# Stick-breaking attention on one core: which engine rounds log(1+e^z) to the matmul format

## Chip, core and metric

The kernel runs on one core of one Trainium2 chip. The metric is the device time of one execution, in microseconds (us). TensorE is called PE, VectorE DVE, ScalarE ACT, GpSimd POOL and SyncE SP.

## What is computed

A two-layer block on one sequence of 512 tokens with 1024 features, in float32. The first layer (pooling and gating mixer, cross attention to 256 memory rows, convolutional FFN of width 2816) ends in a norm. The second layer projects to q, k, v (8 heads of 64) and to a gated convolution of 31 taps over 512 channels, joins attention and convolution in one output product, and ends in a second FFN. The part that matters here is its attention:

```python
z = einsum("bqhd,bkhd->bhqk", qb, kb) * scale           # strictly causal, s < t
log_beta = log_sigmoid(z)
log_one_minus = where(mask, log_sigmoid(-z), 0.0)       # = -log(1 + e^z)
tail = cumsum(log_one_minus, reverse) - log_one_minus   # sum over s < j < t
weights = where(mask, exp(log_beta + tail), 0.0)
out = einsum("bhqk,bkhd->bqhd", weights, vb)
```

## The kernel before

Activations lie with features on the 128 partitions and the 512 tokens along the free axis. Every product runs as three matmuls in a 32-bit matmul format (`fp32r`): an operand is split into `hi`, its rounding to that format, and `lo`, the rest, and hi·hi, hi·lo and lo·hi are added in PSUM (`mm3`, L122 to L125). Weights come in units of 1 MB by SP and are split by ACT (L195) and DVE (L196).

The attention works on four head pairs `hp` = 0 to 3. Each pair has three score tiles `n` = 0, 1, 2, 2x384, 2x384 and 2x512 columns wide (768, 768 and 1024 elements per partition), so there are twelve steps (hp, n). A step has two halves.

- `sticks(hp, n)`: PE writes the scores to a pair of PSUM banks (L774, and the mask at L779). ACT takes Abs, Exp and Ln (L782 to L784), DVE adds max(z, 0) (L785, the "merge"; one operand in PSUM, one in SBUF), and the result log(1+e^z) is split: `hi` by ACT (L131 through `copy_split`), `lo` by DVE (L132, the subtraction, which reads `ex` and `hi` from SBUF).
- `breaks(hp, n)`: PE adds the running sums onto the scores (L798, L801), reading `hi` and `lo`; ACT takes Exp (L803). `gather(hp)` multiplies with the values (L813), and ACT and DVE split the result into `G`.

The same stretch has filler on DVE: the convolution (L832) is done as 120 "taps", one `scalar_tensor_tensor` over 128x512 each, with both tensors in SBUF. `conv_norm` (L877) needs all taps, adds the squares with PE (L882, L895, L904) and gives the operand of the second half of the output product. The first half, `attended` (L941), is 96 matmuls that use `G`.

Each engine runs its instructions strictly in one order. That order is not the order of the source: a scheduler places the instructions of all engines when the program is built, from its own estimate of what each costs, within the data dependences and a few `issue_after` marks. If an operation moves to another engine, the scheduler can place its neighbours differently, too.

```python
        dve.scalar_tensor_tensor(ex, z, 0.0, ex, ALU.max, ALU.add)
        copy_split(*blk(hp, n), ex)
```

Of the kernel before, what the change touches and what calls it, by code (L numbers as in the profile page):

```python
# [10 lines left out]
F32 = mybir.dt.float32  # L11
F32R = mybir.dt.float32r
AF = mybir.ActivationFunctionType
ALU = mybir.AluOpType
# [61 lines left out]
def block_kernel(  # L76
# [12 lines left out]
    pe, act, dve, pool, sp = nc.tensor, nc.scalar, nc.vector, nc.gpsimd, nc.sync  # L89
# [9 lines left out]
    def pair():  # L99
        return psp.tile([P, 2, 512], F32, tag="pp", name="pp")  # L100
# [6 lines left out]
    def t4():  # L107
        return tp.tile([P, 1056], F32, tag="t4", name="t4", bufs=3)
# [10 lines left out]
    def v3(tl, a, b):  # L119
        return tl[:, : a * b].rearrange("p (a b) -> p a b", a=a)  # L120
# [9 lines left out]
    def copy_split(hi, lo, src):  # L130
        act.copy(hi, src)  # L131
        return dve.tensor_tensor(lo, src, hi.bitcast(F32), ALU.subtract)  # L132
# [15 lines left out]
    def part(tl, a, b, at=0):  # L148
        return tl[:, at : at + a * b].rearrange("p (a b) -> p a b", a=a)
# [607 lines left out]
    def cols_of(a):  # L757

        at = 256 if a == 3 else 0
        return slice(at, at + T - a * P)  # L760
# [3 lines left out]
    def sticks(hp, n):  # L764

        w = WIDE[n]
        zt = pair()
        z = zt[:, :, :w]

        for i, (ks, qs) in enumerate(((kT[0], qT[0]), (kT[0], qT[1]), (kT[1], qT[0]))):  # L770
            for a in STEPS[n]:
                for e in range(2):
                    hs = slice(e * HD, (e + 1) * HD)
                    pe.matmul(z[:, e, cols_of(a)], ks[hs, hp, a * P : (a + 1) * P],  # L774
                              qs[hs, hp, a * P :], start=i == 0 and a < 3, stop=False,
                              skip_group_check=True)
        for a in STEPS[n]:
            for e in range(2):
                pe.matmul(z[:, e, cols_of(a)][:, :P], identr, never, start=False, stop=False,  # L779
                          skip_group_check=True)  # L780
        ex = v3(t4(), 2, w)
        act.activation(ex, z, AF.Abs)  # L782
        act.activation(ex, ex, AF.Exp, scale=-1.0)  # L783
        act.activation(ex, ex, AF.Ln, bias=1.0)  # L784
        dve.scalar_tensor_tensor(ex, z, 0.0, ex, ALU.max, ALU.add)  # L785
        copy_split(*blk(hp, n), ex)
        zs[hp, n] = z

    def breaks(hp, n):
# [63 lines left out]
    def place(i):  # L853
        if i not in stk:
            name = ("D0", "B0", "D1", "C0", "C1", "B1", "E1")[i]
            stk[i] = slot(name, F32R if i < 4 else F32)
        return stk[i]

    def blk(hp, n):

        tl = place((hp % 2, 2, 3)[n])
        return tuple(part(tl, 2, WIDE[n], 2 * WIDE[n] * i) for i in range(2))
# [96 lines left out]

    seq = [(hp, n) for hp in range(4) for n in range(3)]  # L960
    sticks(*seq[0])
    sticks(*seq[1])
    project()
    todo = 2
    for i, x in enumerate(seq):

        while todo < len(seq) and todo <= i + 2 and not (x[1] == 2 and seq[todo][1] == 1):
            sticks(*seq[todo])
            todo += 1
        weighted = breaks(*x)  # L970
        if x[1] == 2:
            gather(x[0])
# [130 lines left out]
```

## Time and profile before

| | |
|---|---|
| time, median of 3 runs (lowest to highest) | 1246.66 us (1246.56 to 1247.7) |
| profiled execution: time, and span of its trace | 1246.8 us, 1245.1 us |
| PE busy | 1226.2 us (98%) |
| DVE busy | 771.2 us (62%) |
| ACT busy | 485.2 us (39%) |
| POOL busy | 110.0 us (9%) |

Busy time counts an instruction from its start to its recorded end; matmuls overlap one another, so a busy PE is not PE at its peak. Idle time in front of an instruction is shown in brackets with what ended it. PEld is the loading of weights into PE. "PEclk" is the share of full speed that PE's clock was granted. Times inside the trace are counted from the start of the span.

### The profile page before, as it was taken

The page shows a single profiled execution, that of the slowest core. Times are in us where ns is not written, and L with a number is a line of the kernel's source. Part 1 is how long each engine was busy: PE and PEld are TensorE (multiplying, and loading weights), DVE is VectorE, ACT ScalarE, POOL GpSimd, SP SyncE. Part 2 cuts the span into 40 slices and gives each one's busy share as a digit, 9 for nine tenths or more (in the row PEclk, how much of TensorE's full clock was granted, in tenths as well). Part 3 has the DMA queues.
Part 4 walks back from the last instruction along what each step waited for, and adds up shares of the span by engine and source line. Part 5 has one row for each costly group of instructions (what it writes and reads, how often), then busy time and mean ns, then how long its engine had stood idle before and what let it go on. Part 6 is the DMA issues. An engine that isn't in the chain of part 4 may idle for free.

```text
span 1245.1 us, 13634 instructions
## 1 busy us (share of the span) xinstructions
PE 1226.2 (98%) x5712; PEld 1009.9 (81%) x5712; DVE 771.2 (62%) x813; ACT 485.2 (39%) x528; POOL 110.0 (9%) x125
## 2 busy tenths in 40 slices
PE   8999999999999999999999899999999999999998
PEld 6889888788888888888888778677888888888887
DVE  7855634744766664466375999985775555346532
ACT  6433424623544342243254125873443333223310
POOL 1100210012000000000054412000400000000000
PEclk9999999999999999999999999999999999999999
DMA  8233332312222222222343012201222233223222
GB/s 275 97 106 131 102 102 68 136 68 101 74 97 102 102 102 102 92 83 97 118 152 135 0 35 68 68 1 68 102 99 81 92 102 102 102 102 102 84 68 86
DMA packets 20445, 118.32 MB, mean 95 GB/s; under 512 B 2208, under 2 KB 4128, under 8 KB 7712
## 3 DMA queue, kind: packets, MB, share of 16 engines
q1 hardware_dynamic: 20096, 117.20, 27.4%
q8 instruction: 44, 0.72, 0.2%
q10 hardware_dynamic: 288, 0.26, 0.1%
q14 instruction: 17, 0.14, 0.0%
HBM read 115.35 MB, written 2.10 MB: 94 GB/s over the span
## 4 chain that ended last, share of the span: by engine, by line
PE 92%; DVE 4%; ACT 2%; issue 1%; POOL 1%; DMA 0%; SPq 0%; DVEq 0%; ACTq 0%
PE pp L125 28%; PE pp L123 28%; PE pp L124 28%; DVE H L832 2%; PE ps L123 1%; PE ps L124 1%; PE ps L125 1%; POOL col L739 0%; PE ps L317 0%; DMA A<-in_xT 0%; PE ps L813 0%; DVE t L785 0%; PE pp L774 0%; ACT t L783 0%; PE pp L745 0%
## 5 line engine op out<-in xcount | busy, mean ns | idle before, releaser
L195 ACT CAST whi<-raw 128x2048 fp32r<-128x2048 f32 (+3 forms) x109 | 197.9, 1817 | 425.7 <-PE pp L124 358.5
L196 DVE TENSOR_TENSOR wlo<-raw,whi 128x2048 fp32r<-128x2048 f32 (+3 forms) x109 | 236.7, 2173 | 71.3 <-ACT whi L195 70.7
L123 PE MATMUL pp<-B,whi 128*128 128x512 f32 x672 | 261.7, 390 | 2.4 <-ACT whi L195 2.4
L125 PE MATMUL pp<-B,wlo 128*128 128x512 f32 x672 | 262.1, 390 | 0.2
L124 PE MATMUL pp<-C,whi 128*128 128x512 f32 x672 | 261.8, 390 | 0.0
L124 PE MATMUL pp<-G,whi 128*128 128x512 f32 x448 | 175.1, 391 | 0.0
L125 PE MATMUL pp<-F,wlo 128*128 128x512 f32 x416 | 162.2, 390 | 0.0
L123 PE MATMUL pp<-F,whi 128*128 128x512 f32 x416 | 161.5, 389 | 0.0
L123 PEld LDWEIGHTS pp<-B,whi 128*128 128x128 f32 x672 | 126.2, 188 | 29.3 <-ACT whi L195 3.3
L125 PEld LDWEIGHTS pp<-B,wlo 128*128 128x128 f32 x672 | 126.1, 188 | 27.8 <-DVE wlo L196 1.5
L124 PEld LDWEIGHTS pp<-C,whi 128*128 128x128 f32 x672 | 126.2, 188 | 26.7 <-issue 0.5
L124 PEld LDWEIGHTS pp<-G,whi 128*128 128x128 f32 x448 | 84.1, 188 | 17.6 <-issue 0.2
L625 DVE TENSOR_TENSOR A<-pp,A 128x1024 f32<-128x1024 f32 x23 | 28.2, 1224 | 105.6 <-PE pp L125 105.6
L646 DVE SCALAR_TENSOR_TENSOR H<-H,sm,H 128x512 f32<-128x512 f32 x132 | 92.8, 746 | 0.7
L125 PEld LDWEIGHTS pp<-F,wlo 128*128 128x128 f32 x416 | 78.1, 188 | 16.4 <-issue 0.2
L123 PEld LDWEIGHTS pp<-F,whi 128*128 128x128 f32 x416 | 78.1, 188 | 16.4 <-issue 0.2
L832 DVE SCALAR_TENSOR_TENSOR H<-H,sm,H 128x512 f32<-128x512 f32 x120 | 90.2, 780 | 1.2
L651 DVE TENSOR_TENSOR H<-pp,rb 128x1024 f32<-128x1024 f32 x22 | 26.8, 1224 | 50.6 <-PE pp L125 44.4
L128 ACT ACTIVATE H<-H,sm 128x512 f32<-128x512 f32 x70 | 54.3, 808 | 7.5 <-DVE H L698 7.5
L997 DVE TENSOR_TENSOR H<-pp,rb 128x512 f32<-128x512 f32 x22 | 15.2, 691 | 60.9 <-PE pp L125 54.7
L123 PE MATMUL pp<-D,whi 128*128 128x512 f32 x112 | 43.6, 389 | 0.0
L124 PE MATMUL pp<-E,whi 128*128 128x512 f32 x112 | 43.6, 389 | 0.0
(293 smaller groups left out, 1797.9 us busy)
## 6 DMA issues: line engine op xcount, KB each, us to landing
raw<-in_wts SPq DMA_DIRECT2D x99, 1024.0 KB, 4.8
raw<-in_wts SPq DMA_DIRECT2D x8, 768.0 KB, 4.0
A<-in_xT SPq DMA_DIRECT2D x3, 512.0 KB, 6.8
out<-A SPq DMA_DIRECT2D x3, 512.0 KB, 2.8
D<-in_memT SPq DMA_DIRECT2D x1, 1024.0 KB, 10.7
raw<-in_wts SPq DMA_DIRECT2D x3, 256.0 KB, 7.0
A<-in_xT SPq DMA_DIRECT2D x2, 256.0 KB, 3.9
raw<-in_wts SPq DMA_DIRECT2D x2, 128.0 KB, 4.1
```

Source lines behind the costliest of these rows:

```text
L123: pe.matmul(out, wh, xh, start=start, stop=False, **kw)
L124: pe.matmul(out, wh, xl, start=False, stop=False, **kw)
L125: pe.matmul(out, wl, xh, start=False, stop=stop, **kw)
L128: act.activation(out, in_, AF.Identity, scale=scale, bias=bias)
L195: act.copy(hi[:, cs], raw[:, cs])
L196: dve.tensor_tensor(lo[:, cs], raw[:, cs], hi[:, cs].bitcast(F32), ALU.subtract)
L625: dve.tensor_tensor(hu, pt, hu, ALU.add)
L646: dve.scalar_tensor_tensor(dst, hs[:, k : k + 512], w(k), dst, ALU.mult, ALU.add)
L651: dve.tensor_tensor(hs[:, :, 2:], pt, over2(rb), ALU.mult)
L832: tap = dve.scalar_tensor_tensor(cv[:, i, :], cc[:, i, k : k + 512], par("dw_w", 4 * k + i), cv[:, i, :], ALU.mult, ALU.add)
L997: dve.tensor_tensor(hs[:, 2:514], pt[:, 0, :], rb, ALU.mult)
```

## The change

In `sticks`, the rounding `hi` is written by POOL (`tensor_copy`, a cast from f32 to fp32r), where ACT wrote it. The subtraction stays on DVE; it is the same operation at a new line. All other splits keep ACT.

```diff
         dve.scalar_tensor_tensor(ex, z, 0.0, ex, ALU.max, ALU.add)
-        copy_split(*blk(hp, n), ex)
+        hi, lo = blk(hp, n)
+        pool.tensor_copy(hi, ex)
+        dve.tensor_tensor(lo, ex, hi.bitcast(F32), ALU.subtract)
         zs[hp, n] = z
```

Lines from L787 on are two higher in the changed kernel: the cast is L787, the subtraction L788, and `breaks` has L800, L803 and L805, `gather` L815, the taps L834, `conv_norm` L884 to L911.

The change also moves instructions on DVE and PE. In the names below, `t4_5448`, `t4_5485`, `t4_5542` and `t4_5558` are the results of steps (2,2), (3,0), (3,1) and (3,2), and `pp_5439`, `pp_5468`, `pp_5533` and `pp_5549` their scores in PSUM. `C0_5228`, `B0_5267` and `D1_5095` are the places of `hi` and `lo`, used by one step after another. `H1_2138` is the convolution's result.

DVE in the kernel before, from the merge of step (2,2) on:

```order
L785 SCALAR_TENSOR_TENSOR t4_5448<-pp_5439,t4_5448 128x1024
L832 SCALAR_TENSOR_TENSOR H1_2138<-H0_2137,sm_73,H1_2138 128x512 x3
L132 TENSOR_TENSOR C0_5228<-t4_5448,C0_5228 128x1024
L832 SCALAR_TENSOR_TENSOR H1_2138<-H0_2137,sm_73,H1_2138 128x512
L785 SCALAR_TENSOR_TENSOR t4_5485<-pp_5468,t4_5485 128x768
L832 SCALAR_TENSOR_TENSOR H1_2138<-H0_2137,sm_73,H1_2138 128x512
L785 SCALAR_TENSOR_TENSOR t4_5542<-pp_5533,t4_5542 128x768
L832 SCALAR_TENSOR_TENSOR H1_2138<-H0_2137,sm_73,H1_2138 128x512
L132 TENSOR_TENSOR B0_5267<-t4_5485,B0_5267 128x768
```

The same place in the changed kernel:

```order
L834 SCALAR_TENSOR_TENSOR H1_2138<-H0_2137,sm_73,H1_2138 128x512 x6
L785 SCALAR_TENSOR_TENSOR t4_5448<-pp_5439,t4_5448 128x1024
L834 SCALAR_TENSOR_TENSOR H1_2138<-H0_2137,sm_73,H1_2138 128x512 x4
L788 TENSOR_TENSOR C0_5228<-t4_5448,C0_5228 128x1024
L785 SCALAR_TENSOR_TENSOR t4_5485<-pp_5468,t4_5485 128x768
L788 TENSOR_TENSOR B0_5267<-t4_5485,B0_5267 128x768
L888 SCALAR_TENSOR_TENSOR H1_2138<-ps1_5620,H1_2138 128x512 x4
```

Before, seven taps come behind the subtraction of step (3,0), among the last two steps. Now all taps stand ahead of the subtraction of step (2,2), and `conv_norm` (L888) follows the subtraction of step (3,0) directly.

PE in the kernel before, where `breaks` of step (3,0) begins (`ps0_5522` is the gather of head pair 2):

```order
L801 MATMUL pp_5439<-C0_5228,negtri_89 128x512 x2
L798 MATMUL pp_5468<-B0_5267,negone_87 128x128
L798 MATMUL pp_5533<-B0_5267,negone_87 128x256
L813 MATMUL ps0_5522<-C1_5243,E0_5051 64x512 x2
L774 MATMUL pp_5549<-G0_4674,F0_4900 128x512 x2
L774 MATMUL pp_5549<-G1_4675,F0_4900 128x512 x2
L774 MATMUL pp_5549<-G0_4674,F1_4901 128x512 x2
L779 MATMUL pp_5549<-never_111,identr_94 128x128 x2
L798 MATMUL pp_5468<-B0_5267,negone_87 128x128
L801 MATMUL pp_5468<-B0_5267,negtri_89 128x256 x2
```

The same place in the changed kernel:

```order
L803 MATMUL pp_5439<-C0_5228,negtri_89 128x512 x2
L779 MATMUL pp_5533<-never_111,identr_94 128x128
L884 MATMUL ps1_5620<-H1_2138,ones_83 128x512
L800 MATMUL pp_5468<-B0_5267,negone_87 128x128 x2
L803 MATMUL pp_5468<-B0_5267,negtri_89 128x256 x2
```

The gather of head pair 2 and the scores of step (3,2), which stood ahead of the breaks of step (3,0), now follow them.

PE in the kernel before, at the end of step (3,2), where the last gather (`ps0_5608`) follows eleven matmuls of `attended`, of which three are shown:

```order
L801 MATMUL pp_5549<-C0_5228,negtri_89 128x512 x2
L124 MATMUL pp_5707<-G1_4675,whi_5105 128x512
L125 MATMUL pp_5707<-G0_4674,wlo_5106 128x512
L123 MATMUL pp_5707<-G0_4674,whi_5105 128x512
```

The same place in the changed kernel:

```order
L800 MATMUL pp_5549<-D1_5095,negone_87 128x384 x2
L800 MATMUL pp_5549<-B0_5267,negone_87 128x256 x2
L800 MATMUL pp_5549<-B0_5267,negone_87 128x128 x2
L803 MATMUL pp_5549<-C0_5228,negtri_89 128x512 x2
L906 MATMUL ps1_5651<-t2_5647,ones_83 128x512
L815 MATMUL ps0_5608<-B1_5356,E0_5051 64x512 x2
```

Only one matmul of `conv_norm` is left between the last sums of step (3,2) and the gather that needs their Exp.

## Rows read from the trace of the kernel before

**Rows 1.** Windows: from:to, us, busy us of PE, PEld, DVE, ACT, POOL (instructions), PEclk, DMA.

```profile
780.00:830.00 50.00, 45.74 (x314) 32.34 (x311) 48.67 (x61) 45.18 (x55) 0.00 (x0) 1.00 0.13 43
830.00:858.00 28.00, 28.00 (x128) 21.15 (x127) 17.20 (x25) 10.33 (x13) 1.01 (x1) 1.00 0.11 38
```

**Rows 2.** Waits of PE, 779 to 832 us: us in total, times, longest.

```profile
PE ps L813 <- ACT B L803: 1.4, 1, 1.4
PE pp L798 <- ACT B L131: 1.3, 2, 0.7
```

**Rows 3.** Line L131 on ACT, 765 to 835 us: count, ns min/median/max.

```profile
L131 ACT CAST D<-t x6: 822/830/836, 774.6 to 822.5; 128x768 fp32r<-128x768 f32 x6
L131 ACT CAST C<-t x4: 1039/1047/1053, 787.6 to 830.8; 128x1024 fp32r<-128x1024 f32 x4
```

**Rows 4.** Timeline of POOL: start us, us, instruction.

```profile
0.40 0.10 POOL L1093 MEMSET const-uint8-127<- 128x1 uint8 x1
1.07 0.20 POOL L275 MEMSET t<- 128x128 f32 x1
...
53.54 1.29 POOL L300 TENSOR_TENSOR acc<-t 128x512 f32<-128x512 f32 x1 [13.43 <-ACT t L292]
...
708.38 2.93 POOL L739 TENSOR_TENSOR col<-col,mhalf 128x16 f32<-128x16 f32 x1
```

**Rows 5.** Line L871 on POOL, the whole trace.

```profile
L871 POOL TENSOR_TENSOR A<-A,rb x4: 2414/2862/2955, 680.9 to 689.0; 128x1024 f32<-128x1024 f32 x4
```

**Rows 6.** The taps (L832) beside L871, 680.5 to 692 us.

```profile
L832 DVE SCALAR_TENSOR_TENSOR H<-H,sm,H x2: 2770/2834/2897, 686.7 to 689.6; 128x512 f32<-128x512 f32 x2
```

**Rows 7.** Timeline of DVE, from 679.9 us on: merges of a PSUM operand beside L871.

```profile
679.97 2.35 DVE L693 TENSOR_TENSOR t<-pp,rb 128x1024 f32<-128x1024 f32 x2
```

**Rows 8.** The taps (L832) beside L739, 708 to 712 us.

```profile
L832 DVE SCALAR_TENSOR_TENSOR H<-H,sm,H x5: 737/741/742, 708.9 to 711.6; 128x512 f32<-128x512 f32 x5
```

**Rows 9.** Timeline of DVE, 780 to 832 us.

```profile
781.96 2.29 DVE L196 TENSOR_TENSOR wlo<-raw,whi 128x2048 fp32r<-128x2048 f32 x1 [0.33 <-ACT whi L195]
786.17 1.23 DVE L785 SCALAR_TENSOR_TENSOR t<-pp,t 128x1024 f32<-128x1024 f32 x1 [0.47 <-ACT t L784]
...
817.98 1.22 DVE L132 TENSOR_TENSOR C<-t,C 128x1024 fp32r<-128x1024 f32 x1
819.11 0.75 DVE L832 SCALAR_TENSOR_TENSOR H<-H,sm,H 128x512 f32<-128x512 f32 x1
819.78 0.95 DVE L785 SCALAR_TENSOR_TENSOR t<-pp,t 128x768 f32<-128x768 f32 x1
820.64 0.74 DVE L832 SCALAR_TENSOR_TENSOR H<-H,sm,H 128x512 f32<-128x512 f32 x1
...
825.89 0.68 DVE L132 TENSOR_TENSOR G<-ps,G 128x512 fp32r<-128x512 f32 x1
826.50 3.10 DVE L832 SCALAR_TENSOR_TENSOR H<-H,sm,H 128x512 f32<-128x512 f32 x4
829.52 1.22 DVE L785 SCALAR_TENSOR_TENSOR t<-pp,t 128x1024 f32<-128x1024 f32 x1
830.65 0.74 DVE L832 SCALAR_TENSOR_TENSOR H<-H,sm,H 128x512 f32<-128x512 f32 x1
```

**Rows 10.** Timeline of PE, 820 to 826 us: step (3,0).

```profile
822.68 1.08 PE L813 MATMUL ps<-C,E 128*64 128x512 f32 x4
...
824.86 0.28 PE L798 MATMUL pp<-B,negone 128*128 128x128 f32 x1
```

**Rows 11.** Line L803 on ACT, 815 to 842 us.

```profile
L803 ACT ACTIVATE B<-pp x2: 789/909/1029, 827.1 to 839.2; 128x768 f32<-128x768 f32 x1, 128x1024 f32<-128x1024 f32 x1
```

**Rows 12.** Timeline of PE, 709 to 722 us: an idle time.

```profile
713.97 1.56 PE L745 MATMUL pp<-ident,D 128*128 128x128 f32 x8 [3.64 <-DVE D L741]
```

**Rows 13.** Windows around that idle time, columns as in group 1.

```profile
714.00:720.00 6.00, 3.92 (x18) 3.28 (x19) 5.56 (x8) 1.52 (x2) 2.13 (x2) 0.53 0.01 3
722.00:728.00 6.00, 6.00 (x28) 4.97 (x27) 6.00 (x9) 0.82 (x1) 0.00 (x0) 1.00 0.51 175
```

## The prediction

> **What bounds the kernel now.** I read the busy shares first, then the windows of the attention, then the waits inside them. Over the whole span PE is busy 98% of the time, so a change counts only by what it adds to or takes from PE's idle time. The attention is the exception: from 780 to 830 us PE is busy 45.74 of 50 us, DVE 48.67 and ACT 45.18 [rows 1]. The reader is to see that three engines are nearly full there, DVE most of all, and that POOL does nothing. From 830 us on PE has no idle time, while DVE is busy 17.2 of 28 us. What PE waits for in the attention is mostly ACT: 1.4 us for an Exp and 1.3 us for the rounding that is now moved [rows 2]. So the change takes work from an engine that PE waits for, but the engine without slack is DVE, and its place in the order matters as much as its speed.
>
> **What is removed.** Twelve roundings leave ACT: eight of 768 elements at 0.83 us, of which the rows show six, and four of 1024 at 1.05 us [rows 3], 10.8 us of ACT time. They are worth at most the idle time of PE in that window, 50 − 45.74 = 4.3 us, and only if no other engine takes their place.
>
> **What is added: the price of a rounding on POOL.** The trace has no one-input copy on POOL, so I bound it. Below: a memset, which only writes, takes 0.10 us for 1 element and 0.20 us for 128 [rows 4], 0.8 ns per element; that gives 0.73 us for 768 and 0.94 us for 1024. Above: an addition of two inputs takes 1.29 us for 512 [rows 4] and 2.41 us for 1024, the least of the four L871 [rows 5]; the mean, 1.85 us, serves for 768. These two give 0.17 us fixed and 2.2 ns per element. A copy reads half as much, so I take half the slope: 0.17 + 768 × 1.1 ns = 1.0 us and 1.3 us. That is nearer the lower end, since a copy is nearer to a memset than to an addition.
>
> A page of the Trainium skill puts it lower: by "GPSIMD Engine Reference", Engine selection, an operation with one input runs at roughly line rate, which its table of specifications makes 0.64 and 0.85 us here as an estimate; no run here shows it yet, and with it the sum below would come to 1260.3 us.
>
> **What it does to DVE.** POOL and DVE do not run freely side by side. The taps take 0.74 us elsewhere [rows 8], but the two that ran beside the additions L871 took 2.77 and 2.90 us [rows 6], and each L871 there nearly as much, up to 2.96 us [rows 5]: the two engines took turns, 0.74 us of tap and some 2.1 us of POOL. A tap, like an addition, reads two tensors from SBUF. The merge L785 reads one operand from PSUM, and two such operations took 2.35 us together while the first L871 ran from 680.88 us on [rows 5, 7], no more than the merges of this width take elsewhere [rows 9], so I let it pass. In the new order nearly every merge is followed by a tap, so each rounding waits for the tap that is running and then holds up the next one for its whole length. DVE, which has no slack, grows by that length.
>
> The skill is stricter than the trace here: in "SBUF — State Buffer", Who interferes with whom, whichever engine issues first holds the shared ports for the whole instruction. Rows 8 differ: five taps ran at 0.74 us through a 2.93 us operation on 16 elements [rows 4, 8], so only the streaming part blocks; counting that alone takes 0.17 us per rounding, some 1.5 us, off the sum.
>
> Up to the last tap there are nine roundings, six of 768 and three of 1024: 6 × 1.0 + 3 × 1.3 = 9.9 us. The first is followed by a tap and then by the merge of step (0,1), which covers 0.9 us of it. That leaves **9.0 us** (6.5 us at the lower price, 17.4 us at the upper).
>
> **What is moved, and when step (3,0) is ready.** The orders show that all taps now stand ahead of the subtraction of step (2,2), so that of step (3,0) comes behind the whole convolution. In the trace the last tap ends at 830.65 + 0.74 = 831.39 us [rows 9]. By then DVE had also done what is now later: the 1024 subtraction of (2,2), 1.13 us from start to start; the merges of (3,0) and (3,1), 0.86 us each; their subtractions, 0.87 us each, taken like the merges of that width, since merge and subtraction of 1024 take 1.13 us alike; the split of a gather, 0.61 us; the merge of (3,2), 1.13 us [rows 9]. That is 6.3 us. DVE also sat idle 0.33 and 0.47 us [rows 9], which goes once DVE is the late engine. So without POOL the last tap would end at 831.39 − 6.3 − 0.8 = 824.3 us, and with the 9.0 us at 833.3 us. Then follow the subtraction of (2,2) (1.13), the merge of (3,0) (0.95), its rounding on POOL (0.1 for the handover, 1.0) and its subtraction (0.95): 833.3 + 4.1 = 837.4 us. PE's breaks of step (3,0) need this result.
>
> **What PE pays.** In the trace these breaks start in earnest at 824.86 us, and PE was all but dense from there on [rows 1, 10]. Starting them at 837.4 us costs **12.5 us**. In addition the gather of pair 2 and the scores of (3,2), 822.68 to 824.86 us [rows 10], now stand behind them: **2.2 us**. At the tail, two gathers stand close behind the sums whose Exp they need. The Exp takes 0.80 us in step (3,1) and 1.03 us in (3,2) [rows 11], with 0.1 us for the handover; one has about 0.4 us of short matmuls ahead of it, the other only one matmul of `conv_norm`, again some 0.4 us. That makes 0.5 + 0.7 = **1.2 us**. Before, eleven matmuls covered the last one. `conv_norm` itself starts behind (3,0), and some 60 matmuls of `attended` lie between its last sum and the first product that uses it, so I cost it at nothing; uncovered it would cost its chain of a few us.
>
> PE then waits 3 us and more at a time for DVE. An idle time of 3.64 us [rows 12] was followed by a granted clock of 0.53 from 714 to 720 us, and 1.00 from 722 us on [rows 13]: that is mostly the lower level, 1.2 of 2.4 GHz. If the same comes ahead of step (3,0), work from about 834 to 840 us runs at half rate; part of that is waiting anyway. I bound it by 0 and 2.4 us and take the middle, **1.2 us**, as the waits expected are just about as long as the one seen.
>
> Sum: 12.5 + 2.2 + 1.2 + 1.2 = 17.1 us on the profiled execution of 1246.8 us, which lies 0.1 us above the median of the runs: **1264 us**. With the lower price on POOL and no fall of the clock it is 2.5 + 0.3 + 1.2 = 4.0 us less, 1260 us. With the upper price it is 8.4 us more up to the last tap, 0.85 us more for the rounding of (3,0), and 1.2 us for the full clock: 1274 us.
>
> **The rivals.**
> 1. *The rounding does not hold up DVE.* Rows 8 speak for it: POOL work that hardly reads left the taps alone. Against it: a copy reads all the time, like the additions of rows 5 and 6. Then the 9.0 us and the clock go, and the new order alone stays: 12.5 − 9.0 + 2.2 + 1.2 = 6.9 us, 1254 us. Chance 0.10.
> 2. *Faster: ACT was the bound.* The Exp, Ln and rounding of a step share ACT, which is 90% full, and PE's waits of rows 2 are mostly for it. If the relief lets PE run without a gap, the time is 1246.8 − 4.3 = 1242.5 us. It decides at step (3,0): its subtraction must end by 824.9 us, against 831.39 − 7.1 + 4.1 = 828.4 us even without POOL's turns. Chance 0.04.
> 3. *No change that shows.* PE's gaps shrink early in the attention by about what the late steps cost. A measurement of this kernel tells about 0.2%, 2.5 us, from no change. It needs rival 1 and most of rival 2 together: 1245 to 1249 us. Chance 0.04.
> 4. *The upper price and more:* a cast whose rounding costs POOL extra work per element, above 1.85 us for 768, with a clock that falls in every round of the attention: 1275 us and up. Chance 0.07.
>
> That the change does not do what it says can be left out: the twelve casts stand on POOL and are gone from ACT.
>
> **How the numbers follow.** The forecast, PE held up by DVE with prices between the bounds, has 0.75 and lies from 1260 to 1274 us. With rival 1 and a little above, the range is 1252 to 1275 us; outside it are rivals 2 and 3 and most of 4, some 0.15. Slower is the forecast and rivals 1 and 4: 0.92; the same 0.04, faster 0.04.
>
> **What would show it.** Right: twelve casts on POOL of 1 to 2 us as recorded, waits for the tap included; taps beside them of 1.7 to 2.1 us; the last tap near 833 us; PE busy some 45 of 60 us from 780 to 840 us, waiting for L788 and for casts, with the breaks of (3,0) near 837 us and a clock below 1 in one window or more; PE dense afterwards. Wrong: taps that stay at 0.74 us beside the casts (rival 1); the breaks of (3,0) before 825 us (rival 2); a cast of over 2 us with no tap ahead of it (rival 4).

## The result, and the profile after

The changed kernel takes **1259.59 us** (median; 1258.36 to 1260.44), against 1246.68 us before on the same chip: a ratio of 1.0101, 95% interval 1.0085 to 1.0117. It is 12.9 us slower. The profiled execution has 1260.44 us and a span of 1258.0 us (before: 1245.1 us), again 12.9 us more.

Windows of the changed kernel (from:to, us, busy us of PE, PEld, DVE, ACT, POOL, PEclk, DMA), to be read against [rows 1, 13]:

```profile
780.00:830.00 50.00, 39.58 (x246) 27.75 (x244) 49.01 (x56) 31.22 (x36) 9.52 (x7) 0.87 0.12 43
...
810.00:820.00 10.00, 6.03 (x17) 3.78 (x19) 9.83 (x12) 2.06 (x3) 2.48 (x2) 0.53 0.00 0
828.00:831.00 3.00, 3.00 (x14) 1.58 (x12) 2.93 (x4) 1.50 (x2) 0.17 (x1) 0.50 0.00 0
```

ACT did lose its work: 31.22 us busy from 780 to 830 us, where it had 45.18 (in part because less of the attention falls into the window now: 246 matmuls instead of 314). But DVE is as full as before (49.01), and PE is busy 39.58 us instead of 45.74. The granted clock was 0.53 from 810 to 820 us, where it had been 1.00 throughout. From 828 to 831 us it was down once more, at 0.50, while PE was busy without a gap.

Waits of PE in the changed kernel, 779 to 880 us (us in total, times, longest), against [rows 2]:

```profile
PE pp L803 <- DVE C L788: 5.2, 2, 3.9
PE pp L774 <- ACT C L805: 1.6, 2, 1.2
PE ps L884 <- DVE H L834: 1.5, 1, 1.5
PE ps L815 <- ACT E L805: 1.4, 2, 1.1
```

Before, PE waited mostly for ACT, 1.4 us at a time at most. Now it waits most for a subtraction on DVE, once for 3.9 us, and for a tap; waits for ACT are left beside that.

The casts on POOL and the taps beside them (timelines of POOL and DVE in the changed kernel: start us, us, instruction), against [rows 4, 8, 9]:

```profile
787.47 1.50 POOL L787 CAST C<-t 128x1024 fp32r<-128x1024 f32 x1 [10.95 <-DVE t L785]
...
832.35 0.83 POOL L787 CAST B<-t 128x768 fp32r<-128x768 f32 x1 [4.18 <-DVE t L785]
```

```profile
802.21 3.89 DVE L834 SCALAR_TENSOR_TENSOR H<-H,sm,H 128x512 f32<-128x512 f32 x5
807.15 2.19 DVE L834 SCALAR_TENSOR_TENSOR H<-H,sm,H 128x512 f32<-128x512 f32 x2
810.13 1.97 DVE L834 SCALAR_TENSOR_TENSOR H<-H,sm,H 128x512 f32<-128x512 f32 x2
...
826.52 3.76 DVE L834 SCALAR_TENSOR_TENSOR H<-H,sm,H 128x512 f32<-128x512 f32 x4
830.20 1.22 DVE L788 TENSOR_TENSOR C<-t,C 128x1024 fp32r<-128x1024 f32 x1
831.33 0.95 DVE L785 SCALAR_TENSOR_TENSOR t<-pp,t 128x768 f32<-128x768 f32 x1
833.21 0.96 DVE L788 TENSOR_TENSOR B<-t,B 128x768 fp32r<-128x768 f32 x1 [0.93 <-POOL B L787]
```

The cast at 832.35 us had no tap beside it: 0.83 us is its own length. Those beside taps are recorded at 1.19 to 1.50 us, since, as I read it, they first wait for the tap or the subtraction that is running. Five taps with no cast beside them take 3.89 us; two and four take 1.53 and 3.10 us in the trace of before. Here two take 1.97 us beside a cast of 768 elements (0.44 us more) and 2.19 beside one of 1024 (0.66 us more), and four take 3.76 (0.66 more). Over the nine casts up to the last tap such stretches, one of them of a subtraction, sum to 4.5 us. The last tap ends at 826.52 + 3.76 = 830.28 us, and step (3,0) is ready at 833.21 + 0.96 = 834.17 us.

PE in the changed kernel (timeline), against [rows 10]:

```profile
813.29 0.79 PE L803 MATMUL pp<-C,negtri 128*128 128x512 f32 x1 [3.94 <-DVE C L788]
...
834.89 0.73 PE L800 MATMUL pp<-B,negone 128*128 128x128 f32 x2
```

The breaks of step (3,0) begin at 834.89 us, 10.0 us later than before (824.86). That is 0.7 us behind the subtraction that they need (834.17): PE was still at earlier work, which it had done at half the clock from 828 to 831 us. From there to the end of the span it takes 1258.0 − 834.89 = 423.1 us, where it took 1245.1 − 824.86 = 420.2 us: 2.9 us more.

### The profile page after: what moved, and what is told of

It reads as the page before. It is cut to its first block, busy times and chain, and to the rows that moved or that the text cites. A ratio compares the mean times of both kernels' runs of the same rounds, so it can differ in the third digit from the quotient of the medians.

```text
span 1258.0 us, 13655 instructions
## 1 busy us (share of the span) xinstructions
PE 1232.0 (98%) x5712; PEld 1013.3 (81%) x5712; DVE 775.1 (62%) x813; ACT 476.5 (38%) x516; POOL 126.3 (10%) x137
## 4 chain that ended last, share of the span: by engine, by line
PE 91%; DVE 4%; ACT 2%; issue 1%; POOL 1%; DMA 0%; SPq 0%; DVEq 0%; ACTq 0%
PE pp L124 28%; PE pp L125 28%; PE pp L123 28%; DVE H L834 2%; PE ps L123 1%; PE ps L124 1%; PE ps L125 1%; PE ps L815 1%; DVE t L785 1%; POOL col L739 0%; PE pp L774 0%; PE pp L803 0%; PE ps L317 0%; DVE wlo L196 0%; PE pp L800 0%
## 5 line engine op out<-in xcount | busy, mean ns | idle before, releaser
L834 DVE SCALAR_TENSOR_TENSOR H<-H,sm,H 128x512 f32<-128x512 f32 x120 | 94.2, 813 | 1.4
L646 DVE SCALAR_TENSOR_TENSOR H<-H,sm,H 128x512 f32<-128x512 f32 x132 | 92.8, 747 | 0.7
```

What stands on the lines that cost most here:

```text
L646: dve.scalar_tensor_tensor(dst, hs[:, k : k + 512], w(k), dst, ALU.mult, ALU.add)
L834: tap = dve.scalar_tensor_tensor(cv[:, i, :], cc[:, i, k : k + 512], par("dw_w", 4 * k + i), cv[:, i, :], ALU.mult, ALU.add)
```

## The experiments

### Order and cast taken apart

The change moves a cast and, through the scheduler, the order of everything around it. These runs separate the two. At the end of the kernel's text, a table of instruction numbers (ORDER) ties the instructions of PE, DVE, ACT and POOL, from the attention to the second half of the output product, into the order that they have in one of the two kernels:

```diff
+    traced = {i.name: i for i in tc.nc.cur_bb.bb.instructions}
+    for row in ORDER.strip().split("\n\n"):
...
+        for a, b in zip(names, names[1:]):
+            tc.add_manual_dep(traced[b], a, mybir.DependencyInfo(
+                mybir.DependencyClass.NoSync, mybir.DependencyReason.DATA), reason="order")
```

Such an edge fixes the order of issue on an engine; it adds no wait. The cast itself is left out of the table, but for the two runs that fill a wait and move a subtraction. Line numbers of a kernel with an edit ahead of them are off by one or a few.

**POOL casts, old order.** The changed kernel with the table of the kernel before.

> POOL rounds, but every other instruction of the attention stands in the order of the kernel before. Order-and-turns theory (the new order costs about 8 us, the turns between casts and taps about 4.5 us): only the turns are left, less the 0.8 us for which DVE was idle; 1249 to 1251 us, taps beside casts longer by 0.4 to 0.7 us. Rival, the cast on POOL does it all, whatever the order: 1258 to 1260 us. Rival, the order does it all: 1247 us, or less if the relief of ACT is worth something.

Measured: 1250.23 us, ratio 1.0027 (1.0016 to 1.0038). The first theory's number. DVE's timeline there:

```profile
787.36 2.18 DVE L834 SCALAR_TENSOR_TENSOR H<-H,sm,H 128x512 f32<-128x512 f32 x2
792.13 2.63 DVE L834 SCALAR_TENSOR_TENSOR H<-H,sm,H 128x512 f32<-128x512 f32 x3
811.97 1.31 DVE L834 SCALAR_TENSOR_TENSOR H<-H,sm,H 128x512 f32<-128x512 f32 x1
```

and PE's, at step (3,0):

```profile
827.76 0.28 PE L800 MATMUL pp<-B,negone 128*128 128x128 f32 x1
```

In the kernel before, these groups of two and three taps take 1.53 and 2.19 us, and the single tap 0.74 us: 0.65, 0.44 and 0.57 us more. The last tap ends at 834.91 us instead of 831.39, 3.5 us later, and the time is 3.5 us longer. In the profiled execution PE waits 1.09 us for the cast of step (3,0), its breaks begin in earnest at 827.76 us, 2.9 us later than in [rows 10], and the span is 2.9 us longer (1248.0 us).

**ACT casts, new order.** The kernel before with the table of the changed kernel.

> ACT rounds, but every other instruction of the attention stands in the order of the changed kernel. Order-and-turns theory: the last tap ends 4.5 us before the changed kernel's, near 825.8 us, step (3,0) is ready at 825.8 + 1.13 + 0.95 + 0.93 + 0.95 = 829.8 us, 4.9 us late, with 2.2 us for the work now behind it and 0.6 us of waits at the tail: 1254 to 1256 us, taps 0.74 us each. Rival, the cast on POOL does it all: 1246 to 1248 us. Rival, the order does it all: 1258 to 1260 us.

Measured: 1258.29 us, ratio 1.0094 (1.0079 to 1.0109). No cast is on POOL, and 11.6 of the 12.9 us are there. The order costs more than the first theory said. DVE's last taps, its subtraction of step (3,0), and the PE row of that step:

```profile
823.50 3.10 DVE L832 SCALAR_TENSOR_TENSOR H<-H,sm,H 128x512 f32<-128x512 f32 x4
...
829.71 0.96 DVE L132 TENSOR_TENSOR B<-t,B 128x768 fp32r<-128x768 f32 x1 [0.90 <-ACT B L131]
...
831.09 0.73 PE L798 MATMUL pp<-B,negone 128*128 128x128 f32 x2
```

The last tap ends at 826.60 us, not 825.8, and the breaks of (3,0) begin at 831.09 us, not 829.8.

**No cast, old order.** The merge writes into `hi`:

```diff
-        dve.scalar_tensor_tensor(ex, z, 0.0, ex, ALU.max, ALU.add)
-        copy_split(*blk(hp, n), ex)
+        hi, lo = blk(hp, n)
+        dve.scalar_tensor_tensor(hi, z, 0.0, ex, ALU.max, ALU.add)
+        dve.tensor_tensor(lo, hi.bitcast(F32), ex, ALU.subtract)
```

> No engine rounds: the merge writes its result straight into the place of hi, and the subtraction keeps its size but computes another difference (so the attention's weights are not the reference's). Order of the kernel before. It bounds what freeing ACT of 10.8 us can give. Order-and-turns theory: DVE is the engine without slack, so at most 1 us: 1245.5 to 1247 us. Rival, ACT was the bound: 1242 to 1244 us, PE's idle time between 780 and 830 us mostly gone.

Measured: 1246.93 us, ratio 1.0004 (0.9994 to 1.0013). Taking the cast from ACT and giving it to nobody is worth nothing. The window from 780 to 830 us (columns as above) says why:

```profile
780.00:830.00 50.00, 45.36 (x312) 32.60 (x312) 48.66 (x62) 38.38 (x45) 0.00 (x0) 1.00 0.12 43
```

ACT is 6.8 us less busy than in [rows 1]; DVE and PE are where they were. PE no longer waits 1.3 us for a cast, as in [rows 2]; it waits 3.4 us for DVE, for which it had waited 1.2 us (now 1.2 us for two subtractions, 1.2 us for a merge, 1.0 us for a tap).

**No cast, new order.** The same edit with the table of the changed kernel.

> No engine rounds, as in the run before, in the order of the changed kernel: the order alone, without turns and without waiting for a cast. Order-and-turns theory: 0.9 us earlier at step (3,0) than with ACT's cast in this order: 1253 to 1255 us. Rival, the cast on POOL does it all: 1242 to 1247 us. Rival, the order does it all: 1257 to 1260 us.

Measured: 1255.78 us, ratio 1.0075 (1.0060 to 1.0090), just above the first theory's range. Its last taps and its step (3,0), and a window of the stretch between (columns as above):

```profile
823.35 3.10 DVE L833 SCALAR_TENSOR_TENSOR H<-H,sm,H 128x512 f32<-128x512 f32 x4
...
828.49 0.96 DVE L787 TENSOR_TENSOR B<-B,t 128x768 fp32r<-128x768 f32 x1
...
831.12 0.73 PE L799 MATMUL pp<-B,negone 128*128 128x128 f32 x2
```

```profile
824.00:831.00 7.00, 7.00 (x35) 4.64 (x34) 5.31 (x7) 1.32 (x3) 0.00 (x0) 0.78 0.00 0
```

The subtraction of step (3,0) ends at 829.45 us, but the breaks begin 1.7 us later. PE was busy with earlier work all that time, at a clock of 0.78: by my estimate 7 × 0.22 = 1.5 us of work at full speed were lost there. So most of the 1.7 us may be the clock, though no run isolates it.

Together:

| | no cast | cast on ACT | cast on POOL |
|---|---|---|---|
| old order, median us | 1246.93 | 1246.7 | 1250.23 |
| new order, median us | 1255.78 | 1258.29 | 1259.59 |
| new order: last tap ends, us | 826.45 | 826.60 | 830.28 |
| new order: breaks of (3,0), us | 831.12 | 831.09 | 834.89 |

Each column shows what the order costs: 8.9 us without a cast, 11.6 us with ACT's, 9.4 us with POOL's. Moving the cast costs 3.5 us in the old order. In the new order it puts the last tap off by 3.7 us and step (3,0) by 3.8 us; the medians differ by 1.3 us, and their intervals overlap. The price of the order holds some of the clock: the breaks of (3,0) come behind the subtraction that they need by 1.7 us without a cast, by 0.4 us with ACT's (829.71 + 0.96 = 830.67 us), by 0.7 us with POOL's, each time after a stretch in which the clock was down (0.83 from 820 to 830 us with ACT's cast, too). With ACT's cast the way from (3,0) to the end of the span takes 1255.9 − 831.09 = 424.8 us, with POOL's or none 423.1 us. In that kernel the clock was 0.83 from 840 to 850 us, where the other two had 1.00; I take the 1.7 us to be that, though no run isolates it.

### The turns of POOL and DVE

**Twice the casts.** POOL casts, old order, each cast done twice (`pool.tensor_copy(hi, ex)` repeated).

> POOL rounds each block twice (the second time to the same place with the same value), old order. If each cast takes turns with taps, DVE loses 0.45 to 0.65 us per cast once more, some 4 us up to the last tap, and the wait for the second cast adds up to 0.8 us at steps (1,0) and (3,0), where PE waits for the cast itself: 1253 to 1256 us, and stretches of taps beside a pair of casts grow by 0.9 to 1.3 us. Rival, the 3.5 us of the old order come from the handovers: the second cast adds only its 0.83 to 1.1 us where PE waits, 1251 to 1252.5 us, and the taps stay as they were with one cast.

Measured: 1263.01 us, ratio 1.0128 (1.0114 to 1.0142), above both ranges. The taps did what the first theory said where they ran beside both casts of a pair (DVE's timeline):

```profile
794.50 3.19 DVE L835 SCALAR_TENSOR_TENSOR H<-H,sm,H 128x512 f32<-128x512 f32 x3
825.38 3.63 DVE L835 SCALAR_TENSOR_TENSOR H<-H,sm,H 128x512 f32<-128x512 f32 x3
...
777.40 1.55 DVE L789 TENSOR_TENSOR D<-t,D 128x768 fp32r<-128x768 f32 x1 [1.50 <-POOL D L788]
791.83 1.23 DVE L789 TENSOR_TENSOR C<-t,C 128x1024 fp32r<-128x1024 f32 x1 [0.93 <-POOL C L788]
```

These two groups of three taps take 2.19 and 2.32 us in the kernel before, so two casts of 768 cost 1.0 us and two of 1024 cost 1.3 us: about twice the price of one. The rest is what the expectation missed: the subtraction waits for the second cast, and DVE, which has no slack, stands idle in front of it, 0.93 us at a step of 1024 and 1.5 us where two steps of 768 share POOL. PE in turn waits 3.4 us for the second cast of step (3,0), and the clock was 0.50 from 835 to 845 us behind that; no run tells what each is worth.

**A memset in place of the cast.** Old order:

```diff
-        pool.tensor_copy(hi, ex)
+        pool.memset(hi.bitcast(F32), 0.0)
```

> No engine rounds: POOL writes zeros into the place of hi, a memset of the cast's size, and the subtraction puts the rounded whole into lo (so the products are less exact). Old order. It tells whether POOL's writing alone takes turns with taps. If it is the reading from SBUF: taps 0.74 us beside memsets of 0.73 to 0.94 us, and the time that of the run without a cast, 1246 to 1247.5 us. Rival, writing takes turns too: taps longer by 0.4 us or more, 1248.5 to 1250.5 us.

Measured: 1246.87 us, ratio 0.9997 (0.9988 to 1.0006). POOL's timeline, then DVE's at the same time:

```profile
804.43 0.74 POOL L787 MEMSET D<- 128x768 f32 x1 [12.40 <-PE pp L800]
805.11 0.74 POOL L787 MEMSET B<- 128x768 f32 x1
805.79 0.95 POOL L787 MEMSET C<- 128x1024 f32 x1
```

```profile
803.56 1.53 DVE L834 SCALAR_TENSOR_TENSOR H<-H,sm,H 128x512 f32<-128x512 f32 x2
805.01 0.95 DVE L785 SCALAR_TENSOR_TENSOR t<-pp,t 128x768 f32<-128x768 f32 x1
805.88 0.74 DVE L834 SCALAR_TENSOR_TENSOR H<-H,sm,H 128x512 f32<-128x512 f32 x1
```

Memsets of the cast's size leave the taps at 0.74 us (all 43 of the stretch from 770 to 835 us take 0.74 to 0.75): it is POOL's reading that takes turns with a tap, not its writing. The Trainium skill says the same in "SBUF — State Buffer", Who interferes with whom: a DVE instruction with two inputs in SBUF contends with GpSimd reading SBUF, not with GpSimd only writing it.

### Where in the new order the time is lost

**PE's wait filled.** The changed kernel and its order, with extra matmuls in `breaks` of step (1,2):

```diff
+                    if (hp, n, e, i) == (1, 2, 0, 1):
+                        for _ in range(16):
+                            pe.matmul(out.rearrange("p (a b) -> p a b", a=4), negone,
+                                      over2(identr, 4), start=False, stop=False,
+                                      skip_group_check=True)
```

> The changed kernel in its own order, with 16 extra matmuls of 128x512 on PE in the 3.94 us for which PE waits for the subtraction of step (1,2); each lowers one head's scores by 1, so that head's weights are not the reference's. They take 16 x 0.22 = 3.5 us at full clock and stand where PE would be idle. If the fall of the clock after that wait (0.53 from 810 to 820 us, 0.84 and 0.94 after it) costs time of its own, the clock stays near 1.00 there and the time falls by 3 to 5 us, to 1254.5 to 1256.5 us. Rival, DVE's pace sets the end and PE's slow stretch only fills its waits: 1258.5 to 1260.5 us, with new waits for DVE behind 820 us.

Measured: 1258.55 us, ratio 1.0096 (1.0079 to 1.0113): the rival's number, 1.0 us under the changed kernel (0.6 us by the two ratios), with overlapping intervals. The windows:

```profile
810.00:820.00 10.00, 8.83 (x54) 6.54 (x53) 9.93 (x13) 3.71 (x5) 2.02 (x2) 1.00 0.01 2
820.00:830.00 10.00, 6.91 (x42) 4.30 (x40) 9.72 (x12) 4.95 (x6) 1.43 (x1) 0.83 0.00 0
```

and step (3,0) on DVE and PE:

```profile
832.11 0.96 DVE L788 TENSOR_TENSOR B<-t,B 128x768 fp32r<-128x768 f32 x1 [0.93 <-POOL B L787]
...
833.19 0.73 PE L800 MATMUL pp<-B,negone 128*128 128x128 f32 x2
```

The clock stays at 1.00 from 810 to 820 us, but DVE is as full as before, and PE now waits at 825.56 us, 1.90 us for a merge. The last tap ends at 829.18 us, 1.1 us earlier. The slow stretch had mostly filled time in which PE would have waited for DVE. Only this first stretch is tested: a later one is left (0.83 from 820 to 830 us). It costs nothing here, since the breaks of (3,0) begin at 833.19 us, 0.1 us behind the subtraction that they need (833.07): DVE sets them.

**The subtraction of (1,2) first.** The changed kernel's order; DVE does it ahead of the merge of (2,0) and of two taps, by the table.

> The changed kernel in its own order, but DVE does the subtraction of step (1,2) ahead of the merge of (2,0) and of two taps, and its merge one tap earlier. Nothing is taken away. If the time is lost at that place, PE's wait of 3.94 us shrinks to about 0.5 us and the clock does not fall there: 3.5 us and 1 to 3 us for the clock, 1253 to 1256 us. Rival, as the prediction had it, the last tap and step (3,0) set the end: the last tap stays near 830.3 us, the breaks of (3,0) near 834.9 us, 1258.5 to 1260 us.

Measured: 1259.78 us, ratio 1.0113 (1.0085 to 1.0140), from four executions of 1258.12 to 1266.01 us. PE's timeline:

```profile
810.84 0.50 PE L803 MATMUL pp<-C,negtri 128*128 128x512 f32 x1 [0.74 <-DVE C L788]
...
816.03 0.39 PE L800 MATMUL pp<-D,negone 128*128 128x256 f32 x1 [2.66 <-DVE t L785]
```

The wait of 3.94 us fell to 0.74, and 2.66 us came back at the next merge. The last tap ends at 827.36 + 3.76 = 831.1 us and the breaks of (3,0) begin at 836.17 us, 1.2 us behind the subtraction that they need (835.00), after a stretch at half the clock (0.50 from 827 to 833 us). The rival's view holds: the sum of DVE's work ahead of step (3,0) sets the time, not the place of one wait; the 1.2 us behind it may be the clock's, though no run isolates them.

### An order with late taps

**ACT casts, late taps.** If early taps cost time, later ones might gain some. The table of the kernel before, with one to five taps put off on DVE, the last five behind the subtraction of (3,2).

> ACT rounds, order of the kernel before on PE, but DVE's taps are put off: one less ahead of step (0,2)'s subtraction, then two, three, four, and five taps behind the subtraction of step (3,2), where DVE sat idle for 4.1 us. If taps ahead of the subtractions of steps (hp, 2) are what holds PE, this is the opposite of the changed kernel's order and must be faster than before: PE's waits for those subtractions (0.4 and 0.6 us) and for the merge (0.2 us) go, perhaps some of the other 2.7 us: 1244 to 1246 us. Rival, the chain through ACT sets the pace: no change, 1246.7 us. Slower only if conv_norm, now later, is no longer covered.

Measured: 1249.60 us, ratio 1.0018 (1.0009 to 1.0027): slower, against the expectation. PE's timeline and the window that shows why:

```profile
820.48 0.33 PE L798 MATMUL pp<-B,negone 128*128 128x128 f32 x1 [0.61 <-ACT B L131]
822.22 0.38 PE L798 MATMUL pp<-B,negone 128*128 128x256 f32 x1 [1.41 <-DVE t L785]
```

```profile
780.00:830.00 50.00, 45.02 (x292) 32.52 (x292) 44.55 (x55) 43.74 (x53) 0.00 (x0) 0.93 0.12 43
820.00:830.00 10.00, 8.11 (x32) 5.92 (x33) 7.60 (x11) 7.02 (x9) 0.00 (x0) 0.66 0.00 0
```

The waits for the subtractions of (1,2) and (2,2) are gone, and DVE is relieved (44.55 us instead of 48.67). But PE waits elsewhere, 0.7 us more in all (45.02 us busy instead of 45.74), and behind two waits of 0.61 and 1.41 us the granted clock was 0.66 from 820 to 830 us. The span grew by 2.8 us: 0.7 us are idle time, and I put the other 2.1 us down to the clock, though no run isolates them. The executions bear out most of it: the seven with a mean clock of 0.994 took 1249.59 to 1250.46 us, the four with 0.996 took 1248.25 to 1248.57 us, 1.6 us less by their medians, and still above the kernel before. From 822.22 to 885 us PE has no further wait in which a slow stretch could hide.

**POOL casts, late taps.** The same table for the changed kernel.

> POOL rounds, in the same order with late taps. If POOL's price is only the turns on a full DVE, the five taps put off (5 x 0.73 = 3.6 us) give back what the turns took (3.5 us in the old order): 1246 to 1248 us. Rival, the price is the longer chain through POOL at each step: it stays near 1250 us.

Measured: 1250.62 us, ratio 1.0028 (1.0018 to 1.0038). That is the rival's number, but it can't decide, since the order itself turned out 2.7 us slower: against ACT's cast in this order POOL's costs 1.0 us, with overlapping intervals. PE waits 2.2 us for POOL's casts there, where it waited 1.2 us for ACT's, and 3.4 us for DVE, where it waited 2.2: the waits of both theories grew. Neither version beats the kernel before.

## Why the prediction was right, and where it was not

The direction held, and 1259.59 us lies in the range of 1252 to 1275, just below the 1260 to 1274 us of the forecast itself. The way to it held too: DVE is the engine without slack, relief of ACT is worth nothing, and the time is set by when DVE, with all taps ahead, gets step (3,0) done (to within the 0.1 to 1.7 us by which PE came behind it in the runs in this order). Two of its sizes were wrong, in opposite directions, so that the total was close in part by luck. Of its signs, casts of 1.19 to 1.50 us beside taps were seen, and a PE that is nearly dense behind step (3,0). Taps of 1.7 to 2.1 us were not: casts held them up by 0.44 to 0.66 us. The last tap and step (3,0) came 2 to 3 us earlier than named.

| term of the sum | predicted, us | measured, us |
|---|---|---|
| breaks of (3,0) late by the order, without POOL | 828.4 − 824.86 = 3.5 | 831.1 − 824.86 = 6.2 |
| later still by POOL's turns | 9.0 | 834.89 − 831.1 = 3.8 |
| gather and scores now behind, waits at the tail | 2.2 + 1.2 | 423.1 − 420.2 = 2.9 |
| clock ahead of (3,0) | 1.2 | within these; at most 834.89 − 834.17 = 0.7 |
| sum | 17.1 | 12.9 |

- **The price of a cast: nearly right.** Taken: 1.0 us for 768 elements; the one cast that ran alone in the changed kernel took 0.83 us, between the lower end (0.73) and the value taken. In the run with twice the casts one of 1024 elements ran alone and took 1.04 us. These two lengths give 0.8 ns per element and 0.2 us fixed, where 1.1 ns and 0.17 us were taken. The Trainium skill's rule in "GPSIMD Engine Reference", Engine selection (line rate for one input, by my estimate 0.64 us) is 0.2 us too low here.
- **The turns: the step that failed.** "Each rounding waits for the tap that is running and then holds up the next one for its whole length." The first half is seen: casts beside taps are recorded at up to 1.50 us. The second is not: taps were held up by 0.44 to 0.66 us, some 53 to 69% of a cast's own length. The total was 4.5 us of stretched work, and 3.7 to 3.8 us at the last tap, where 9.0 us were forecast; 3.7 to 3.8 us is also what the runs in the new order show between POOL's cast and ACT's or none. From the operation on 16 elements the prediction had named a fixed part of 0.17 us that doesn't block, and left it out of the sum. (Four of the five taps of [rows 8] ran beside that operation; the fifth began at 711.6 us, when it had ended at 711.31.) The runs put the part at 0.83 − 0.57 = 0.26 to 0.83 − 0.44 = 0.39 us.
- **The order without POOL: too cheap.** The last tap was put at 824.3 us; the runs without POOL's cast have it at 826.45 and 826.60. The prediction took 0.8 us off for idle time "which goes once DVE is the late engine". It does not go: from 772 us to the last tap DVE is idle 2.7 us in the run without a cast (51.72 of 54.45 us busy) and 1.8 us before (57.59 of 59.40). In that run it waits 0.78 us for the split of a weight on ACT and 0.62 us for PE, which, held up by DVE, hands its scores over late in turn. Of the 2.7 us that this row of the table lacked, some 2.3 us stand at the last tap. The other 0.4 us stand behind it, where PE, in the run with ACT's cast, began the breaks that much after the subtraction.
- **What stands behind step (3,0): right.** 2.9 us. The two waits of PE at the tail came to 0.32 and 0.26 us, 0.6 us in all instead of 1.2, and 0.40 us for the subtraction of step (3,1), which the sum did not have, came beside them. That leaves 1.9 us for the gather and the scores moved behind (2.2 predicted).
- **The clock: seen, and cheap.** A wait of 3.94 us was followed by a clock of 0.53, as [rows 12, 13] had suggested, but at step (1,2). With that wait filled and the clock up there, the time changed by 1.0 us, within the intervals. A second stretch, 0.50 from 828 to 831 us, did come ahead of (3,0), as forecast, though behind a wait of only 1.2 us for an Exp. It put the breaks off by 0.7 us at most, as PE would else have waited for DVE.
- **The rivals.** Rival 1 (casts don't hold up DVE) falls, since taps stretch; its 1254 us are near the 1255.8 us of the new order without a cast. Rival 2 (ACT was the bound) falls most clearly: no cast at all gives 1.0004 in the old order. Rival 3 (no change) falls with the ratio, 1.0085 at least. Rival 4 falls with the cast of 0.83 us.

So the errors, 5.2 us too much for POOL and 2.7 us too little for the order, offset each other in part. Most of the loss is the order, which no line of the change names.

## What to carry to other kernels

Before an operation is moved off a busy engine, run the kernel with the operation left out: if that gains nothing, no new place for it can in the same order. Where a scheduler sets the order, compare the orders, and run the old one with the new engine and the new one with the old engine before either is blamed. Work on POOL that reads SBUF is paid for by DVE's work with two SBUF operands beside it, so look at what DVE has to spare.

## What the runs showed of the hardware

- A cast of 128x768 from f32 to fp32r on POOL takes 0.83 us, the same as on ACT [rows 3]; it holds up a DVE tap beside it by 0.44 to 0.57 us, one of 128x1024 by 0.66 us. Alone, a cast of 128x1024 takes 1.04 us (in the run with twice the casts). Memsets of 0.74 and 0.95 us hold up none.
- The merge, with one operand in PSUM, was not held up: the one of 768 elements at 774.22 us in the changed kernel, beside a cast from 773.71 us on, took 0.95 us, as in [rows 9], and so did the one at 774.01 us with POOL's casts in the old order. No merge of 1024 ran beside a cast in the changed kernel.
- The clock fell behind short waits, too: with ACT's casts and late taps it was 0.66 from 820 to 830 us, with idle times of 0.61 and 1.41 us, while the kernel before kept 1.00 through 0.61, 0.72 and 0.22 us at the same place.
